# Nine diagonal matrices for the first norm, made by VectorE in place of ScalarE

## The chip, the cores and the metric

The kernel runs on one core of one Trainium2 chip. The metric is the device time of one execution in microseconds (us), as the median of several runs. The times are taken without the profiler; one more execution is recorded by the hardware profiler, and it is the one that the views show.

## What is computed

The reference is one step of a one-layer hybrid encoder, for 1024 prompt frames and 32 sample frames (1056 columns in all), model width 1024. Cut to what matters here:

```python
def rmsnorm(x, g):
    y = xf * lax.rsqrt(jnp.mean(xf * xf, axis=-1, keepdims=True) + EPS)
    return y * g

h = rmsnorm(x, g_mix)
proj = h @ w_in
q, k, v, cb, cc, cx, ga, gc = jnp.split(proj, SPLITS, axis=-1)
...
```

What follows (attention, a short convolution, gates, an output projection, a squared-ReLU MLP, a gated embedding and a last norm) is not touched by the change.

## The kernel before

The data are kept by feature: features lie on the 128 partitions, frames along the columns. The first norm is not applied ahead of the projection. The kernel multiplies the weights with `x * g_mix`, and scales each finished product by the frame's factor 1/rms, which must then stand in every partition: the tile `rs`, 128 x 1056. Its making is the place of the change.

The functions `stats_x` (L397) and `spread` (L384) make it. `stats_x` takes nine blocks of frames by rows (eight of 128, one of 32), lets ScalarE sum the squares of each (L403, into a column of `ssq`), takes the root on ScalarE (L408) and the reciprocal on VectorE (L409). The result `rst` has a frame per partition and a block per column. `spread` is then called three times, for three blocks each. For a block it scales the identity by the block's column of `rst`, which gives a diagonal matrix `dg` (L391), and multiplies it with a matrix of ones on TensorE (L392), which puts each frame's factor into all partitions of a column of the PSUM tile `pr`. When the three blocks of a call are there, ScalarE copies `pr` into `rs` (L394). The tile `dg` has four buffers and `pr` two. An fp32 matmul shows as two passes in the trace, so nine blocks give 18 records.

The order of the work is written by hand: within `manual_schedule` every engine runs its instructions in the order of the program. The main work is a list of matrix products, `seven` (L208), seven block products per pair of weight tiles, with each product's sum split in a high and a low part (three matmuls, L202 to L204). The output of a product leaves PSUM through a copy of ScalarE (L227, L231, L235, L647) or an operation of VectorE (L238, L243, L248). After each product, `run` advances every generator in the list `side` by one step: `prepare` makes the next weights' parts (adds on GpSimd, L189; casts on ScalarE, L150 and L97; differences on VectorE, L152 and L98), `fetch_in` issues loads on SyncE's queue (L88), and `stats_x` is one of these generators too. All three calls of `spread` lie in its last step, between two products of `seven`: behind the copy L231 of the second product `S1` and ahead of the product into `ps_A11i` that follows.

At the end of the kernel, `diagonals` (L1635) and `everywhere` (L1644) do the same for the later norms in blocks of 100 or 128 frames (L1641, L1649); the change doesn't touch them. The function `inv_rms`, which calls `spread` too, isn't used.

Of the kernel before, what the change touches and what calls it, by code (L numbers as in the profile page):

```python
# [11 lines left out]
AF = mybir.ActivationFunctionType  # L12
ALU = mybir.AluOpType
# [35 lines left out]
def tile_step(  # L49
# [8 lines left out]
    nc = tc.nc  # L58
# [13 lines left out]
    ident = cpool.tile([P, P], F32, name="ident")  # L72
# [311 lines left out]
    def spread(r9, dst, q0):  # L384

        w = min(3 * P, T - q0 * P)
        pr = tps.tile([P, 512], F32, tag="tp", name="pr")
        for i in range(q0, q0 + 3):
            n = P if i < 8 else DEC
            dg = cpool.tile([P, P], F32, tag="dg", name="dg", bufs=4)  # L390
            nc.scalar.activation(dg, ident, AF.Copy, scale=r9[:, i : i + 1])  # L391
            nc.tensor.matmul(pr[:, (i - q0) * P : (i - q0) * P + n], ones, dg[:, :n], start=True, stop=True)  # L392
        if dst is not None:
            nc.scalar.copy(dst[:, q0 * P : q0 * P + w], pr[:, :w])  # L394
        return pr[:, :w]

    def stats_x():  # L397

        nc.vector.memset(ssq, 1.0)
        for i in range(9):  # L400
            n = P if i < 8 else DEC
            r = rows[i % 3][:n, :]
            nc.scalar.activation(r, r, AF.Square, accum_out=ssq[:n, i : i + 1])  # L403
            if i < 6:
                load_rows(i + 3)
            for _ in range(3 if i in (2, 5) else 1):
                yield
        nc.scalar.activation(rst, ssq, AF.Sqrt, bias=eps_t, scale=1.0 / D)  # L408
        nc.vector.reciprocal(rst, rst)  # L409
        for _ in range(3):  # L410
            yield
        for q0 in (0, 3, 6):
            spread(rst, rs, q0)
# [668 lines left out]
    with tc.manual_schedule(engines=MM):  # L1082
# [3 lines left out]
        for n in range(len(steps) + 3):  # L1086
            done_f, parts = 0, None
            w0, w1 = (pace_ + [FILL])[n : n + 2]
            if n < len(steps):
                i = steps[n][2]  # L1090
# [53 lines left out]
    def inv_rms(src, r, name, square=False):  # L1144
        r9 = cpool.tile([P, 9], F32, name=f"r9{name}")
        nc.vector.memset(r9, 1.0)
        row_rms(src, r9, range(9), name, square)
        for q0 in (0, 3, 6):
            spread(r9, r, q0)
# [793 lines left out]
```

## Time and profile before

| | us |
|---|---|
| median of 3 runs | 1547.47 |
| lowest and highest | 1547.33, 1547.64 |
| the profiled execution | 1547.13 |
| its span in the profile | 1545.4 |
| mean granted clock of TensorE | 0.998 |

The span runs from the first to the last instruction; the profiled execution's own time is 1.7 us longer, which lies around the span. In the views, PE is TensorE, PEld its weight loads, DVE is VectorE, ACT is ScalarE, POOL is GpSimd and SP is SyncE, which issues the transfers. Tiles are shown by name without their number, so the product tiles of this stage are `ps_A11i`, `ps_A12i` and `ps_S1i`. A bracket at the end of a line of the timeline tells how long the engine was idle before it and whose instruction ended that. Ends of matmuls are modelled and overlap the next start, so the pace of TensorE is read from starts.

### The profile page before, as it was taken

Reading aid. Unit: us, or ns where it says so; the run is one execution under the profiler, and the core shown is the slowest. Engines: PE = TensorE matmul, PEld = TensorE weight load, DVE = VectorE, ACT = ScalarE, POOL = GpSimd, SP = SyncE. Lnnn points to the kernel's source line nnn. Section 1 sums busy time; section 2 is a strip of 40 time slices with the busy share of each in tenths; the row PEclk is TensorE's granted clock in tenths of the full one; section 3 lists DMA queues with packets and bytes.
Section 4 is the critical chain, followed back from the end, with each engine's and each line's share of the span. In section 5 each row is a group of like instructions: output and inputs, shape, how many; then the busy total and the mean of one; then the engine's idle time right before and its main releaser. Section 6 shows DMA issues by size and latency. Waiting matters only on the chain.

```text
span 1545.4 us, 29349 instructions
## 1 busy us (share of the span) xinstructions
PE 1521.4 (98%) x11786; PEld 1507.2 (98%) x11786; DVE 1058.1 (68%) x1385; ACT 759.7 (49%) x1393; POOL 347.2 (22%) x294
## 2 busy tenths in 40 slices
PE   8999999999999999999999999999999999999997
PEld 8999999999999999999999999999999999999997
DVE  7524686667688887766577555544576986789856
ACT  6652344443566775333355555555543333434656
POOL 1122232230211114002312222221020221013453
PEclk9999999999999999999999999999999999999999
DMA  6522245534735576235454344344886897683443
GB/s 243 180 93 84 56 166 193 205 132 121 224 113 156 157 229 236 90 137 170 162 189 145 143 150 151 132 142 154 282 303 202 275 337 242 195 282 108 141 133 111
DMA packets 111559, 269.10 MB, mean 174 GB/s; under 512 B 13472, under 2 KB 29216, under 8 KB 111424
## 3 DMA queue, kind: packets, MB, share of 16 engines
q1 hardware_dynamic: 110704, 265.05, 51.0%
q8 instruction: 92, 1.51, 0.4%
q10 hardware_dynamic: 720, 2.19, 0.4%
q14 instruction: 43, 0.35, 0.1%
HBM read 186.46 MB, written 80.73 MB: 173 GB/s over the span
## 4 chain that ended last, share of the span: by engine, by line
PE 92%; DVE 4%; ACT 2%; issue 1%; DMA 0%; SPq 0%; POOL 0%; DVEq 0%; ACTq 0%; POOLq 0%
PE ps_dn L1473 7%; PE ps_dn L1472 7%; PE ps_dn L1474 7%; PE ps_A11u L203 4%; PE ps_A11u L202 4%; PE ps_A11u L204 4%; PE ps_A11i L202 4%; PE ps_A11i L204 4%; PE ps_A11i L203 4%; PE av L874 2%; PE ps_wo L106 2%; PE ps_wo L107 2%; PE ps_wo L108 2%; PE ps_S1u L203 2%; PE ps_S1u L202 2%; PE ps_S1u L204 2%
## 5 line engine op out<-in xcount | busy, mean ns | idle before, releaser
L1473 PE MATMUL ps_dn<-fl,whi_dn 128*128 128x264 f32 x896 | 254.8, 284 | 0.1
L1474 PE MATMUL ps_dn<-fh,wlo_dn 128*128 128x264 f32 x896 | 254.9, 284 | 0.0
L1472 PE MATMUL ps_dn<-fh,whi_dn 128*128 128x264 f32 x896 | 254.8, 284 | 0.0
L1473 PEld LDWEIGHTS ps_dn<-fl,whi_dn 128*128 128x128 f32 x896 | 168.5, 188 | 0.3 <-DVE fl L1381 0.3
L1472 PEld LDWEIGHTS ps_dn<-fh,whi_dn 128*128 128x128 f32 x896 | 168.6, 188 | 0.0
L1474 PEld LDWEIGHTS ps_dn<-fh,wlo_dn 128*128 128x128 f32 x896 | 168.6, 188 | 0.0
L189 POOL TENSOR_TENSOR s_i<-raw_i,raw_i 128x512 f32<-128x512 f32 x30 | 40.4, 1346 | 232.8 <-DVE slS_i L152 210.4
L1365 DVE TENSOR_TENSOR wlo_dn<-raw_dn,whi_dn 128x1024 fp32r<-128x1024 f32 x40 | 71.0, 1774 | 25.7 <-ACT whi_dn L1359 25.1
L1359 ACT CAST whi_dn<-raw_dn 128x1024 fp32r<-128x1024 f32 x40 | 42.1, 1052 | 93.7 <-PE ps_dn L1473 79.5
L819 DVE TENSOR_TENSOR_SCAN r<-r 128x128 f32<-128x128 f32 (+3 forms) x64 | 86.6, 1354 | 2.1 <-POOL r L812 2.1
L189 POOL TENSOR_TENSOR s_u<-raw_u,raw_u 128x512 f32<-128x512 f32 x30 | 44.7, 1491 | 186.3 <-DVE slS_u L152 185.6
L1414 POOL TENSOR_TENSOR c<-c,rs 128x528 f32<-128x528 f32 x16 | 26.7, 1669 | 244.1 <-DVE c L1481 122.6
L1381 DVE TENSOR_TENSOR fl<-mr,fh 128x1056 fp32r<-128x1056 f32 x56 | 69.7, 1247 | 4.1 <-ACT fh L1376 4.1
L152 DVE TENSOR_TENSOR slS_i<-s_i,shS_i 128x512 fp32r<-128x512 f32 x45 | 36.0, 802 | 49.2 <-ACT shS_i L150 49.0
L202 PE MATMUL ps_A11i<-T,shS_i 128*128 128x264 f32 x240 | 69.0, 287 | 0.2 <-ACT u_i L235 0.2
L203 PE MATMUL ps_A11i<-T,shS_i 128*128 128x264 f32 x240 | 68.6, 286 | 0.0
L204 PE MATMUL ps_A11i<-T,slS_i 128*128 128x264 f32 x240 | 68.4, 285 | 0.0
L202 PE MATMUL ps_A11u<-T,shS_u 128*128 128x264 f32 x240 | 68.4, 285 | 0.0
L203 PE MATMUL ps_A11u<-T,shS_u 128*128 128x264 f32 x240 | 68.3, 285 | 0.0
L204 PE MATMUL ps_A11u<-T,slS_u 128*128 128x264 f32 x240 | 68.1, 284 | 0.0
L812 POOL TENSOR_SCALAR_AFFINE_SELECT r<-r 128x128 f32<-128x128 f32 x64 | 26.6, 416 | 165.2 <-ACT r L805 165.1
L1376 ACT CAST fh<-mr 128x1056 fp32r<-128x1056 f32 x56 | 60.1, 1073 | 5.0 <-DMA mr<-mdB 5.0
(462 smaller groups left out, 5591.8 us busy)
## 6 DMA issues: line engine op xcount, KB each, us to landing
raw_dn<-in_w_down_dram SPq DMA_DIRECT2D x56, 512.0 KB, 4.7
raw_i<-in_w_in_dram SPq DMA_DIRECT2D x34, 512.0 KB, 4.4
mr<-mdT SPq DMA_DIRECT2D x32, 528.0 KB, 5.4
raw_u<-in_w_up_dram SPq DMA_DIRECT2D x32, 512.0 KB, 3.5
mdB<-m SPq DMA_DIRECT2D x48, 264.0 KB, 2.4
mr<-mdB SPq DMA_DIRECT2D x24, 528.0 KB, 6.5
s<-gd SPq DMA_DIRECT2D x16, 528.0 KB, 5.4
mdT<-ta SPq DMA_DIRECT2D x32, 264.0 KB, 2.1
```

Source lines behind the costliest of these rows:

```text
L189: f()
L202: nc.tensor.matmul(p_, wh[:, k, :], o[:, 0, c], start=new and n == 0, stop=False, **on)
L203: nc.tensor.matmul(p_, wh[:, k, :], o[:, 1, c], start=False, stop=False, **on)
L204: nc.tensor.matmul(p_, wl[:, k, :], o[:, 0, c], start=False, stop=z, **on)
L819: nc.vector.tensor_tensor_scan(rev, rev, rev, 1.0, ALU.mult, ALU.bypass)
L1359: nc.scalar.copy(hi, dws[u])
L1365: dve(lo, raw, hi.bitcast(F32), op=sub)
L1376: nc.scalar.copy(h, mraw[v])
L1381: dve(l, mraw.pop(v), opd[v].bitcast(F32), op=sub)
L1472: nc.tensor.matmul(ps, hi[:, j, :], oh, start=j == 0, stop=False)
L1473: nc.tensor.matmul(ps, hi[:, j, :], ol, start=False, stop=False)
L1474: nc.tensor.matmul(ps, lo[:, j, :], oh, start=False, stop=j == NP_ - 1)
```

## The change

One line of `spread` is replaced. The scaled identity is made by VectorE's `tensor_scalar` with a multiply, from the same operands, instead of ScalarE's `activation` with a scale. Nothing else is changed: the position in the program, the four buffers of `dg`, the matmuls and the copies stay. VectorE's nine instructions take the place of ScalarE's nine in the program's order.

```diff
             dg = cpool.tile([P, P], F32, tag="dg", name="dg", bufs=4)
-            nc.scalar.activation(dg, ident, AF.Copy, scale=r9[:, i : i + 1])
+            nc.vector.tensor_scalar(dg, ident, r9[:, i : i + 1], None, op0=ALU.mult)
             nc.tensor.matmul(pr[:, (i - q0) * P : (i - q0) * P + n], ones, dg[:, :n], start=True, stop=True)
```

## The prediction

> **What bounds the kernel now.** I read the page first, then the waits of TensorE, then the order of time around the edited line. The page:
>
> ```profile
> span 1545.4 us, 29349 instructions
> ...
> PE 1521.4 (98%) x11786; PEld 1507.2 (98%) x11786; DVE 1058.1 (68%) x1385; ACT 759.7 (49%) x1393; POOL 347.2 (22%) x294
> ...
> PE 92%; DVE 4%; ACT 2%; issue 1%; DMA 0%; SPq 0%; POOL 0%; DVEq 0%; ACTq 0%; POOLq 0%
> ```
>
> TensorE is busy for 98% of the span, and 92% of the chain that ended last is its work. So time that TensorE loses anywhere is lost at the end, and the question is only what it loses at the nine diagonals. The waits of TensorE between 84 and 300 us have one large entry (total, times, longest), and it is the edited line:
>
> ```profile
> PE pr L392 <- ACT dg L391: 2.5, 3, 0.9
> ```
>
> Those 2.5 us are idle time only. Inside the three groups TensorE also runs at the pace of the diagonals, which the timeline shows (start, duration, engine, line):
>
> ```profile
> 83.79 0.29 PE L203 MATMUL ps_S1i<-T,shS_i 128*128 128x264 f32 x1
> 83.91 0.28 PE L204 MATMUL ps_S1i<-T,slS_i 128*128 128x264 f32 x1
> 84.23 0.38 ACT L231 COPY s_i<-ps_S1i 128x264 f32<-128x264 f32 x1 [1.08 <-PE ps_S1i L204]
> 84.50 0.98 ACT L391 ACTIVATE dg<-ident,rst 128x128 f32<-128x128 f32 x3
> 84.96 1.07 PE L392 MATMUL pr<-dg,ones 128*128 128x128 f32 x6 [0.77 <-ACT dg L391]
> 86.07 0.48 ACT L394 COPY rs<-pr 128x384 f32<-128x384 f32 x1 [0.58 <-PE pr L392]
> 86.44 0.98 ACT L391 ACTIVATE dg<-ident,rst 128x128 f32<-128x128 f32 x3
> 86.90 1.07 PE L392 MATMUL pr<-dg,ones 128*128 128x128 f32 x6 [0.87 <-ACT dg L391]
> 88.00 0.48 ACT L394 COPY rs<-pr 128x384 f32<-128x384 f32 x1 [0.58 <-PE pr L392]
> 88.38 0.98 ACT L391 ACTIVATE dg<-ident,rst 128x128 f32<-128x128 f32 x3
> 88.84 1.49 PE L392 MATMUL pr<-dg,ones 128*128 128x128 f32 x6 [0.87 <-ACT dg L391]
> 90.14 0.57 PE L202 MATMUL ps_A11i<-T,shS_i 128*128 128x264 f32 x1
> ```
>
> This is a ping-pong. ScalarE can begin the diagonals only after its copy of the product just finished (L231), makes three, waits until TensorE has used them, copies the result out (L394), and only then makes the next three. The products before follow each other every 0.12 us (83.79 to 83.91), so TensorE could have gone on at 84.03; the next product starts at 90.14. The stretch costs 6.11 us for 18 passes (each fp32 matmul is two).
>
> A second loss follows. The windows show the granted clock (length, PE busy, PEclk, DMA share, GB/s), and two starts of products bound it:
>
> ```profile
> 88.60:88.80 0.20, 0.00 (x0) 1.00 0.00 0
> 88.80:89.00 0.20, 0.16 (x1) 0.53 0.00 0
> 92.00:92.20 0.20, 0.20 (x3) 0.50 0.00 0
> 92.20:92.40 0.20, 0.20 (x4) 0.94 0.00 0
> ...
> 92.25 0.29 PE L202 MATMUL ps_A11i<-T,shS_i 128*128 128x264 f32 x1
> 94.08 0.28 PE L202 MATMUL ps_A12i<-B,whi_i 128*128 128x264 f32 x1
> ```
>
> From 88.8 to 92.2 us the clock is at half. From 92.25 to 94.08 stand 15 starts, 0.122 us each; the nine before them, from 90.14 to 92.25, took 2.11 us in place of 9 x 0.122 = 1.10. So the drop cost 1.01 us after the stretch, besides what it cost within it.
>
> **The change part by part.** It removes nine instructions of ScalarE and puts nine of VectorE in the same place of the program:
>
> ```profile
> L391 ACT ACTIVATE dg<-ident,rst x9: 388/389/403, 84.5 to 89.0; 128x128 f32<-128x128 f32 x9
> L1680 DVE TENSOR_SCALAR yl<-yl,r 128x512 f32<-128x512 f32 x1 | 0.5, 486 | 0.0
> L1682 DVE TENSOR_SCALAR yl<-yl,r 128x256 f32<-128x256 f32 x2 | 0.7, 346 | 0.0
> L555 DVE TENSOR_SCALAR cs<-ce,vecT 128x2 f32<-128x2 f32 x4 | 0.9, 221 | 0.0
> ```
>
> *One diagonal on VectorE.* No row has this operation at 128 columns. From 256 to 512 columns it grows by 140 ns, so 128 columns give 346 - 70 = 276 ns. The bounds are the rows of 2 columns (221 ns) and of 512 (486 ns). I take 0.28 us, for both neighbours lie on that line.
>
> *When they can start.* VectorE's timeline around the place, with POOL's:
>
> ```profile
> 80.66 0.21 DVE L409 RECIPROCAL rst<-rst 128x9 f32<-128x9 f32 x1 [1.09 <-ACT rst L408]
> 81.17 0.69 DVE L152 TENSOR_TENSOR slS_i<-s_i,shS_i 128x512 fp32r<-128x512 f32 x1 [0.29 <-ACT shS_i L150]
> 93.75 0.69 DVE L152 TENSOR_TENSOR slA_i<-raw_i,shA_i 128x512 fp32r<-128x512 f32 x1 [11.89 <-ACT shA_i L150]
> ...
> 82.00 1.28 POOL L189 TENSOR_TENSOR s_i<-s_i,raw_i 128x512 f32<-128x512 f32 x1 [1.00 <-DVE slS_i L152]
> 102.72 1.28 POOL L189 TENSOR_TENSOR s_i<-raw_i,raw_i 128x512 f32<-128x512 f32 x1 [19.43 <-DVE slS_i L152]
> ```
>
> The factor is ready at 80.87, and VectorE idles from 81.86 to 93.75. Its next work, the L152 of 93.75, needs a cast that ScalarE issues after the spread, so the diagonals are queued ahead of it. Four buffers hold diagonals, so four are made from about 81.9 to 83.0, while TensorE still multiplies. The first three waits go; they are covered by VectorE's idle time.
>
> *What is late next.* A fully fed pass is seen at the end of the kernel, where the diagonals are all made before the matmuls start:
>
> ```profile
> 1445.09 0.34 PE L108 MATMUL ps_pg<-bh,wlo_pg 128*128 128x400 f32 x1
> 1445.27 1.03 PE L1649 MATMUL pr<-dg,ones 100*128 100x100 f32 x8
> ...
> L1649 PE MATMUL pr<-dg,ones x36: 249/275/353, 1445.3 to 1519.1; 100*128 100x100 f32 x32, 128*128 128x128 f32 x4
> ```
>
> Eight passes in 1.03 us with 0.275 for one: (1.03 - 0.275)/7 = 0.108 us between starts. With 128 columns it may be up to the 0.12 of the products. From 84.03, 18 x 0.108 = 1.94 us end at 85.97; by 0.12, at 86.19. Two waits can remain in it:
> - The fifth diagonal needs the buffer of the first, that is the end of pass 2 (84.14 + 0.275 = 84.41). With 0.05 us to VectorE, 0.28 for itself and 0.07 to TensorE (84.96 less the first diagonal's end at 84.50 + 0.39), it is there at 84.81; pass 9 is due at 84.89. The others follow every 0.28 while a pair of passes takes 0.216: the ninth, there at 85.93, is about 0.06 late.
> - The third group writes the buffer of the first, which ScalarE must have copied out (two buffers): pass 6 ends at 84.57 + 0.275 = 84.85, the copy takes 0.48 from 84.89 to 85.37, TensorE may write at 85.44, and pass 13 is due at 85.33. Cost 0.11.
>
> These overlap, so the next product starts at about 86.1 instead of 90.14: **4.0 us** gained. Bounds: 4.16 with no wait and 0.108; and, with the 0.49 of the 512-column row for a diagonal, the ninth is there at 84.46 + 5 x 0.49 + 0.07 = 86.98, the product starts at 87.2, and 2.9 are gained.
>
> *The clock.* The drop came at 88.8, and in the 3.4 us before it TensorE sat idle twice for 0.87. Fed without those gaps, passes keep the clock:
>
> ```profile
> 1445.00:1448.00 3.00, 3.00 (x27) 2.96 (x26) 2.61 (x6) 2.16 (x6) 0.00 (x0) 1.00 0.41 99
> ```
>
> Here the same kind of passes ran with clock 1.00. I take it that the drop goes: another **1.0 us**. Bounds: from a full drop that stays (3.4 us at half, 1.7 lost: 0.7 worse than now) to 1.0 gained. Here a rule of the Trainium skill speaks against me: "TensorE: Matmul & The Clock Gate", Part 1, says that the clock is halved after an idle window of about 3.4 us, and that the windows run free of the kernel. The length agrees (88.8 to 92.2 is 3.4 us), the cause does not quite: the longest idle here was 0.87 us. By that rule the waits did not cause the drop and it would stay, which is my second case.
>
> *What lies behind.* ScalarE loses nine times about 0.3 us here, of no worth in itself; its copies follow TensorE. Does the gain survive to the end? At the stretch the kernel has run dry:
>
> ```profile
> 84.00:94.00 10.00, 7.49 (x44) 6.92 (x43) 0.25 (x1) 5.56 (x16) 0.00 (x0) 0.83 0.00 0
> ...
> 94.47 1.85 SPq L88 DMA_DIRECT2D raw_i<-in_w_in_dram  x2
> ```
>
> DMA share 0.00, POOL nothing, VectorE nothing before 93.75, and the next loads wait for buffers that VectorE frees. All that follows hangs on TensorE's products, so it moves as one block. POOL's add of 82.00 lies beside the first diagonals; if one waits for the other, a diagonal is up to 1.28 us late: then the fourth is there at 83.28 + 4 x 0.28 + 0.07 = 84.47, due at 84.68, and nothing is lost.
>
> **Sum.** 4.0 + 1.0 = 5.0 us. The profiled execution took 1547.13 (1.7 beyond its span), so 1542.1; by the median of the runs, 1547.47, it is 1542.5. I take the middle, **1542.3 us**, 0.33% less.
>
> **The rivals.**
> 1. *The clock still drops.* The pauses go, but a 3.4 us stretch at half clock falls on dense products and loses 1.7: gain 5.0 - 1.7 = 3.3, so 1543.8 to 1544.2. For: the passes use narrow tiles, and what the clock looks at isn't seen. Against: the row of 1445 with clock 1.00.
> 2. *The diagonals pace TensorE.* At 0.49 us each, gain 2.9 + 1.0 = 3.9, so 1543.2 to 1543.6. For: the fifth waits for a buffer. Against: two rows put it at 0.28.
> 3. *The lead is given back.* A later wait that doesn't move eats over 1.9 us, leaving the time above 1544.4. For: TensorE does wait elsewhere in 1540 us. Against: everything was idle at the stretch, so no transfer or engine was ahead that could now be caught up with.
> 4. *Slower.* Each of diagonals five to nine waits out one add of POOL (1.28, as the row of 82.00) before its own 0.28. Then the ninth is there at 84.46 + 5 x 1.56 + 0.07 = 92.3, the product starts at 92.5, 2.4 us later than now: 1549.5. It decides from 1.1 us each (84.46 + 5 x 1.1 = 90). Against: POOL has one add between 82.00 and 102.72. The Trainium skill, "SBUF — State Buffer", Who interferes with whom, states that such an operation of VectorE and any of GpSimd can shut each other out of a shared port for a whole instruction; no row here shows these two side by side.
>
> **How the numbers follow.** A measurement of this kernel can tell about 0.2%, 3.1 us, from no change: below 1544.4 counts as faster. Chances: the forecast 0.68, the dropping clock 0.13, the pacing 0.11, the lead given back 0.06, slower 0.02. The first three are all faster (0.92). The range runs from 1540.9 (4.16 + 1.0, and up to 1 us more where a run's drop fell wholly on dense products) to 1544.2, the upper ends of rivals 1 and 2.
>
> **What the next profile would show.** Nine DVE instructions at L391 of about 0.28 us, four before 83.1; one unbroken group of 18 passes from 84.0 with no wait over 0.2; the next product near 86.1; the granted clock 1.00 from 86 to 93; the two copies L394 near 84.9 and 86; span near 1540.4. Wrong would be: a diagonal of 0.4 or more with waits of TensorE on VectorE, a half-clock window behind 86, or an equal span with a new wait between the stretch and the end.

## The result

The changed kernel takes 1542.91 us (median of 8 runs, 1542.00 to 1543.91); the kernel before, measured beside it, 1547.95 (8 runs, 1546.15 to 1549.15). The ratio is 0.9967, with a 95% interval from 0.9957 to 0.9978: 5.0 us faster, clear of no change. The profiled execution took 1543.23 us, with a span of 1541.5. The forecast was 1542.3 us and a gain of 5.0.

### The profile page after: what moved, and what is told of

Its sections match the earlier page's. It is cut to its first block, busy times and chain, and to the rows that moved or that the text cites. A ratio compares the mean times of both kernels' runs of the same rounds, so it can differ in the third digit from the quotient of the medians.

```text
span 1541.5 us, 29349 instructions
## 1 busy us (share of the span) xinstructions
PE 1520.1 (99%) x11786; PEld 1506.4 (98%) x11786; DVE 1061.1 (69%) x1394; ACT 756.8 (49%) x1384; POOL 347.1 (23%) x294
## 4 chain that ended last, share of the span: by engine, by line
PE 92%; DVE 4%; ACT 2%; issue 1%; DMA 0%; SPq 0%; POOL 0%; DVEq 0%; ACTq 0%; POOLq 0%
PE ps_dn L1473 7%; PE ps_dn L1472 7%; PE ps_dn L1474 7%; PE ps_A11u L203 4%; PE ps_A11u L202 4%; PE ps_A11u L204 4%; PE ps_A11i L202 4%; PE ps_A11i L204 4%; PE ps_A11i L203 4%; PE av L874 2%; PE ps_wo L106 2%; PE ps_wo L107 2%; PE ps_wo L108 2%; PE ps_S1u L203 2%; PE ps_S1u L202 2%; PE ps_S1u L204 2%
## 5 line engine op out<-in xcount | busy, mean ns | idle before, releaser
L1473 PE MATMUL ps_dn<-fl,whi_dn 128*128 128x264 f32 x896 | 255.0, 285 | 0.1
L1473 PEld LDWEIGHTS ps_dn<-fl,whi_dn 128*128 128x128 f32 x896 | 168.6, 188 | 0.3 <-DVE fl L1381 0.3
```

The source lines that it names most:

```text
L1473: nc.tensor.matmul(ps, hi[:, j, :], ol, start=False, stop=False)
```

## The profile after

The page of the changed kernel has nine instructions more on VectorE and nine fewer on ScalarE, and TensorE's share is up by a point:

```profile
span 1541.5 us, 29349 instructions
...
PE 1520.1 (99%) x11786; PEld 1506.4 (98%) x11786; DVE 1061.1 (69%) x1394; ACT 756.8 (49%) x1384; POOL 347.1 (23%) x294
```

The timeline around the edited line, of all engines (start, duration, engine, line):

```profile
82.45 1.90 DVE L391 TENSOR_SCALAR dg<-ident,rst 128x128 f32<-128x128 f32 x4
82.67 1.40 POOL L189 TENSOR_TENSOR s_i<-s_i,raw_i 128x512 f32<-128x512 f32 x1 [1.00 <-DVE slS_i L152]
...
84.59 0.28 PE L204 MATMUL ps_S1i<-T,slS_i 128*128 128x264 f32 x1
84.71 2.25 PE L392 MATMUL pr<-dg,ones 128*128 128x128 f32 x18
85.12 1.18 DVE L391 TENSOR_SCALAR dg<-ident,rst 128x128 f32<-128x128 f32 x5 [0.78 <-PE pr L392]
85.57 0.48 ACT L394 COPY rs<-pr 128x384 f32<-128x384 f32 x1 [0.29 <-PE pr L392]
86.24 0.48 ACT L394 COPY rs<-pr 128x384 f32<-128x384 f32 x1 [0.19 <-PE pr L392]
...
86.80 0.37 PE L202 MATMUL ps_A11i<-T,shS_i 128*128 128x264 f32 x1
87.00 0.40 ACT L394 COPY rs<-pr 128x288 f32<-128x288 f32 x1 [0.27 <-PE pr L392]
...
89.80 0.29 PE L202 MATMUL ps_A12i<-B,whi_i 128*128 128x264 f32 x1
```

Where three groups of six passes stood with a pause ahead of each, one group of 18 stands, with one short wait inside it: fed passes start every 0.11 us (84.71 to 85.93 for the first twelve), and the 13th, the first of the third group, starts at 86.11, 0.06 us late, behind the first copy (85.57 + 0.48 = 86.05). Four diagonals are ready before TensorE reaches them. From the last start of the product `S1` to the next product it is 86.80 - 84.59 = 2.21 us, where it was 90.14 - 83.91 = 6.23: **4.02 us** gone (0.47 of it by the third group, whose last passes ran at half clock before: 1.30 us from its start to the next product in before, 0.83 where the clock holds, as in e4 below). The 24 starts behind it, from 86.80 to 89.80, take 3.00 us, where they took 3.94 (90.14 to 94.08): **0.94 us** gone. The windows tell why (length; busy time and count of PE, PEld, DVE, ACT, POOL; granted clock, DMA share, GB/s):

```profile
86.00:93.00 7.00, 7.00 (x59) 6.91 (x59) 2.64 (x6) 3.58 (x8) 0.00 (x0) 1.00 0.23 73
```

The clock is 1.00 throughout. Together 4.96 us are gained in this place. The span is only 3.9 us shorter, since in this execution the product `S1` ended 0.68 us later than in that of before, ahead of the changed place, and 0.4 us differ in the 1450 us behind it. The lead holds to the end. The row of the later norms' matmuls, of the changed kernel, has the first start at 1441.3, where it was 1445.3 before, and the last at 1515.2, where it was 1519.1:

```profile
L1649 PE MATMUL pr<-dg,ones x36: 249/275/353, 1441.3 to 1515.2; 100*128 100x100 f32 x32, 128*128 128x128 f32 x4
```

## The experiments

Two theories stand against each other. **Theory 1**: the loss was one of place. The diagonals stood in ScalarE's queue behind copies that wait for TensorE, so the two engines took turns, and the pauses brought the clock down. **Theory 2**: the engine counts, because VectorE's instruction is shorter (0.28 against 0.39 us) or because ScalarE has less to do. For each kernel I give the time from the last start of `S1` to the next product ("stretch") and to the first start of `ps_A12i`, 24 starts later ("with products"); before has 6.23 and 10.17, the changed kernel 2.21 and 5.21.

### e1: the diagonals stay on ScalarE, earlier in its queue

Nothing is left out; the diagonals are written into row tiles that are no longer used, so none waits for a buffer.

```diff
+    ready = []
+    def make_ready(*blocks):
+        for i in blocks:
+            dg = rows[i // 8][:, i % 8 * P : (i % 8 + 1) * P]
+            nc.scalar.activation(dg, ident, AF.Copy, scale=rst[:, i : i + 1])
+            ready.append(dg)
...
-        for _ in range(3):
-            yield
+        for q0 in (0, 3, 6):
+            yield
+            make_ready(q0, q0 + 1, q0 + 2)
```

In `spread`, `dg = ready[i]` takes the place of the two lines that made it.

> The nine diagonals stay on ScalarE, with the same instruction, but stand earlier in its queue: three behind each of the three products ahead of the spread, written into the row tiles that are free by then, so none waits for a buffer. Theory 1 (place in the queue: the diagonals stood behind copies that wait for TensorE, and the pauses brought the clock down): the first two groups run without a wait; the first copy L394 stands behind the last three diagonals (to about 85.9 on the scale of before), so the third group is some 0.6 late; the next product starts 2.6 to 2.8 us after the last start of S1 in place of 6.2; the clock keeps 1.00; 4.2 to 4.7 us faster than before, about 1543.5. Theory 2 (the engine: VectorE's diagonal is shorter and ScalarE has less to do): ScalarE does the same work in the same time, so under 1 us is gained, 1547 to 1548.

Measured: 1543.96 us (1543.41 to 1544.48), ratio to before 0.9967, 0.9954 to 0.9979; before in these runs 1549.24. Stretch 2.69 (84.42 to 87.11), with products 5.69. The timeline of e1:

```profile
82.09 0.99 ACT L401 ACTIVATE xr<-ident,rst 128x128 f32<-128x128 f32 x3
...
83.55 0.99 ACT L401 ACTIVATE xr<-ident,rst 128x128 f32<-128x128 f32 x3
84.54 1.50 PE L391 MATMUL pr<-xr,ones 128*128 128x128 f32 x12
...
85.02 0.98 ACT L401 ACTIVATE xr<-ident,rst 128x128 f32<-128x128 f32 x3
85.90 0.84 ACT L393 COPY rs<-pr 128x384 f32<-128x384 f32 x2
86.42 0.85 PE L391 MATMUL pr<-xr,ones 128*128 128x128 f32 x6 [0.38 <-ACT rs L393]
```

ScalarE does as many diagonals, each as long as before, and nearly all of the gain is there. By the medians it is 5.3 us, more than the 4.2 to 4.7 expected, since most runs of before beside it have a mean clock of 0.996. Theory 2 falls. The one wait left, 0.38 us, is that of the third group for the first copy, which stands behind the last three diagonals: place in the queue again.

### e7: nine on ScalarE at the old place, ahead of the copies

As e1, with `make_ready(*range(9))` at the place of the old diagonals.

> All nine diagonals on ScalarE at the place of before, but ahead of the three copies instead of three and three between them, into row tiles that are free. Theory 1 (place in the queue): the first pause stays (0.77), TensorE is then paced by a diagonal every 0.3 us, the first copy stands behind the ninth diagonal (87.2 on the scale of before) and the third group behind that copy (87.7): 4.4 to 4.6 us from the last start of S1 to the next product in place of 6.2, so 1.7 us faster where before's clock does not drop (1546.4), 1544.5 to 1545.5. Theory 2 (the engine): ScalarE's work is unchanged, so the time of before.

Measured: 1544.95 us (1544.38 to 1546.77), ratio 0.9982, 0.9973 to 0.9991; before in these runs 1548.65. Stretch 4.43 (83.93 to 88.36), with products 7.44.

```profile
84.52 2.74 ACT L401 ACTIVATE xr<-ident,rst 128x128 f32<-128x128 f32 x9
84.98 1.95 PE L391 MATMUL pr<-xr,ones 128*128 128x128 f32 x12 [0.77 <-ACT xr L401]
87.16 0.83 ACT L393 COPY rs<-pr 128x384 f32<-128x384 f32 x2
87.67 0.85 PE L391 MATMUL pr<-xr,ones 128*128 128x128 f32 x6 [0.75 <-ACT rs L393]
```

Same engine, same nine instructions; what differs is their order among the copies, and that they are written into free row tiles, so nine can be made without a buffer to wait for. The stretch is 1.80 us shorter than in the profile of before, and 1.32 shorter than in e2 (5.75), which takes the old turns at full clock. The first pause stays, since the first diagonal is still behind the copy of `S1`; a second stands where the copy is late. The clock stayed at 1.00 with two pauses of 0.77 and 0.75 us (more on that below).

### e4: only the first call's diagonals on VectorE

```diff
+            if q0 == 0:
+                nc.vector.tensor_scalar(dg, ident, r9[:, i : i + 1], None, op0=ALU.mult)
+            else:
+                nc.scalar.activation(dg, ident, AF.Copy, scale=r9[:, i : i + 1])
```

> Only the first call's three diagonals are made by VectorE; the other six stay on ScalarE. Theory 1: the first group starts with no wait and with no gap inside, the first copy L394 and the two calls behind it come 1.2 us earlier, and their two pauses stay: the stretch is 5.0 in place of 6.2 us. Whether two pauses bring the clock down is open: 1.2 us faster than before if it drops, 2.2 to 2.6 if it doesn't; 1545.3 to 1546.8. Theory 2 (the work taken off ScalarE counts): a third of 5.0, 1.7 us, spread evenly, with the first pause as long as before.

Measured: 1544.98 us (1544.73 to 1545.77), ratio 0.9977, 0.9966 to 0.9987; before 1549.24. That is 4.3 us by the medians, more than expected; the time itself lies just under the expected range. In the profile the stretch is 4.58 (85.08 to 89.66) and with products 7.58, so 2.59 us less than in the profile of before: the second group starts 1.81 after the last start of `S1` where it was 2.99 (1.18, as forecast), and the clock gives 0.47 in the third group and 0.94 behind it. The rest of the 4.3 lies in the runs of before, whose clock drop mostly costs more than in its profile (below). The waits of TensorE for ScalarE are now two:

```profile
PE pr L395 <- ACT dg L394: 1.7, 2, 0.9
```

### e3: one buffer for the diagonals

```diff
+    one = [cpool.tile([P, P], F32, tag="dg", name="dg", bufs=4)]
...
-            dg = cpool.tile([P, P], F32, tag="dg", name="dg", bufs=4)
+            dg = one[0]
```

> The changed kernel with a single buffer for the diagonals, so each waits until TensorE has used the one before. The prediction's terms for a round trip: 0.07 to TensorE, 0.108 to the second pass, 0.275 for it, 0.05 back, 0.28 for the diagonal, about 0.78 us for each. Theory 1: nine on VectorE in this order cost 8 x 0.78 + 0.22 = 6.5 us from the last start of S1 to the next product, 0.3 more than before, and with TensorE busy for 0.22 of 0.78 the clock drops again and may stay low for two windows of 3.4 us: 1547.5 to 1550. Theory 2 (the engine): the instructions and their engine are those of the changed kernel, so its 1543 stays within 1 us.

Measured: 1550.62 us (1550.15 to 1552.08), ratio to before 1.0013, 1.0004 to 1.0022, so 7.7 above the changed kernel. VectorE does the same nine instructions and the whole gain is lost, and more. Stretch 7.55 (84.95 to 92.50), with products 12.97. One round of it in the timeline:

```profile
85.83 0.49 PE L394 MATMUL pr<-dg,ones 128*128 128x128 f32 x2 [0.38 <-DVE dg L393]
86.36 0.28 DVE L393 TENSOR_SCALAR dg<-ident,rst 128x128 f32<-128x128 f32 x1 [0.58 <-PE pr L394]
86.69 0.49 PE L394 MATMUL pr<-dg,ones 128*128 128x128 f32 x2 [0.38 <-DVE dg L393]
```

The windows of e3 in which the clock falls and rises again:

```profile
91.00:92.00 1.00, 0.58 (x2) 0.30 (x2) 0.32 (x2) 0.00 (x0) 0.00 (x0) 0.68 0.00 0
...
97.00:98.00 1.00, 1.00 (x7) 1.00 (x6) 0.75 (x2) 0.36 (x1) 0.00 (x0) 0.50 0.00 0
98.00:99.00 1.00, 1.00 (x9) 1.00 (x9) 0.62 (x1) 0.84 (x2) 0.00 (x0) 0.91 0.63 139
```

A round takes 0.86 us, not the 0.78 of the prediction's terms: the hand-overs are 0.04 and 0.05 us and the diagonal 0.28, but a pair of passes that starts on an idle TensorE takes 0.49 instead of 0.108 + 0.275. The stretch is so 1.0 us longer than the 6.5 expected, and the time lies 0.6 above the expected range. The clock is at half from about 91.4 to 98.2, 6.8 us, twice the length seen before. The prediction's slower rival is another mechanism (it needed POOL's adds); what e3 shows is that a round trip that TensorE must wait out can cost more than the old turn-taking.

### e2: the pauses filled, not shortened

Four matmuls are added ahead of each group; their result is overwritten.

```diff
+        for _ in range(4):
+            nc.tensor.matmul(pr[:, :P], ones, ident, start=True, stop=True)
```

> The kernel before, with four additional matmuls of the ones and the identity into pr ahead of each group of three, overwritten by the real ones, to fill TensorE's pauses without shortening them (four fp32 matmuls are eight passes, 0.86 us by 0.108; the pauses are 0.77 to 0.87). Theory 1 (the pauses bring the clock down): the three waits for ScalarE stay but the clock stays at 1.00; the 24 products behind the stretch take 2.95 us in place of 3.94 and the third group 1.07 in place of 1.49, together 1.4 us faster than before, about 1546.5. Rival (the clock drops for another reason than the pauses): half clock for 3.4 us appears as before, the same time as before or up to 1 us longer.

Measured: 1546.61 us (1546.29 to 1548.14), ratio 0.9986, 0.9978 to 0.9995; before 1549.24. Stretch 5.75 (84.14 to 89.89), with products 8.75: 1.42 us less than in the profile of before, by the clock alone. The timeline of e2:

```profile
84.26 1.05 PE L389 MATMUL pr<-ident,ones 128*128 128x128 f32 x8
...
84.74 0.98 ACT L393 ACTIVATE dg<-ident,rst 128x128 f32<-128x128 f32 x3
85.19 1.07 PE L394 MATMUL pr<-dg,ones 128*128 128x128 f32 x6
86.10 1.06 PE L389 MATMUL pr<-ident,ones 128*128 128x128 f32 x8
```

And the window of it in which the clock of before fell:

```profile
88.00:90.00 2.00, 2.00 (x17) 1.83 (x17) 0.00 (x0) 1.36 (x4) 0.00 (x0) 1.00 0.00 0
```

The turn-taking goes on as before, every diagonal at its old time, and the clock holds. Ten of the eleven runs of e2 have a mean clock of 0.999; of the 24 runs of before beside them, three have it. So the pauses did bring the clock down, and its cost is separate from theirs.

### e5, e9, e10, e11: the kernel before again

The times of before spread over 4 us. In one set of 21 runs beside the second group of experiments they follow the mean granted clock: 1546.1 us at 0.999 (three runs), 1547.1 to 1548.7 at 0.998 (six), 1548.5 to 1549.4 at 0.996 and 0.997 (twelve). Elsewhere the order is looser: three runs of e5 at 0.997 took 1547.2 to 1547.4 us, and e2 spreads from 1546.3 to 1548.1 with 0.999 in ten of eleven runs, so some of the spread has another place, which no trace here shows. These four runs of the unchanged kernel look for the place of the clock's part.

> The kernel before, unchanged, in another execution. Its runs lie between 1546.4 us at a mean granted clock of 0.999 and 1550.3 at 0.996. Theory 1 on the clock (the pauses bring it down, but what it costs depends on where the 3.4 us windows fall): same groups and the same 6.2 us from the last start of S1 to the next product within 0.4, but a half-clock stretch that begins elsewhere or lasts two windows (6.8 us) where the mean clock is 0.996 or 0.997, with up to 3.4 us lost on the products behind. Rival (the spread of the times comes from another place): the same stretch of 3.4 us as before, and the difference in span lies elsewhere.

> The kernel before, unchanged, one more look, in search of an execution whose mean granted clock is 0.996 or 0.997. Theory 1 on the clock: if it is 0.996, half clock lasts about 6.8 us here (two stretches of 3.4), the products behind the stretch lose about 3 us and the span is near 1547.5; if 0.998, one stretch as in the profile of before. Rival: at 0.996 the half-clock time lies elsewhere in the kernel.

> The kernel before, unchanged, one more look with the same question: two stretches of 3.4 us at half clock behind the pauses where the mean clock is 0.996, one where it is 0.998, none where it is 0.999.

> The kernel before, unchanged, one more look with the same question: two stretches of 3.4 us at half clock behind the pauses where the mean clock is 0.996, one where it is 0.998, none where it is 0.999.

Measured: e5 1547.29 us (median of 10 runs, ratio to the other runs of before 0.9994, 0.9985 to 1.0003), the others one execution each.

| | time of the profiled run | mean clock | stretch | with products | half clock |
|---|---|---|---|---|---|
| profile of before | 1547.13 | 0.998 | 6.23 | 10.17 | 88.8 to 92.2 |
| e5 | 1547.03 | 0.998 | 6.02 | 10.24 | about 88.9 to 92.3 |
| e11 | 1548.07 | 0.998 | 5.91 | 10.30 | about 89.8 to 93.2 |
| e9 | 1549.25 | 0.997 | 6.67 | 11.22 | about 87.8 to 94.6 |
| e10 | 1549.22 | 0.996 | 6.54 | 11.25 | about 88.2 to 95.0 |

The two ends of the half clock in the windows of e10:

```profile
88.00:89.00 1.00, 1.00 (x6) 0.74 (x4) 0.00 (x0) 0.19 (x1) 0.00 (x0) 0.60 0.00 0
89.00:90.00 1.00, 0.13 (x2) 0.10 (x1) 0.00 (x0) 0.93 (x3) 0.00 (x0) 0.50 0.00 0
94.00:95.00 1.00, 1.00 (x6) 1.00 (x6) 0.00 (x0) 0.77 (x2) 0.00 (x0) 0.50 0.00 0
95.00:96.00 1.00, 1.00 (x10) 1.00 (x9) 0.69 (x1) 1.00 (x2) 0.00 (x0) 0.98 0.00 0
```

The clock is at half for 3.4 us or for 6.8. Against e2, which has the same turns at full clock (8.75), the drop costs 1.4 to 1.6 us in the one case and 2.5 in the other, its share within the groups included. Behind the stretch, the 24 starts take 4.55 us in e9 and 4.71 in e10 in place of 3.00, so they lose 1.6 and 1.7 us, not the 3 expected. In e9 and e10 the clock falls within the second group, so that the pause ahead of the third lies in the first 3.4 us at half clock, as a pause of e3 does; in the other three traces at most 0.03 us of a pause is left when it falls. An execution of before with 0.999 has no trace here; that its clock never drops in this place is inferred from its time, 1546.1, which is near that of e2's fastest (1546.29).

### e6: the diagonals of VectorE made at once

All nine are made on VectorE behind the reciprocal, into the row tiles, as in e1 with `nc.vector.tensor_scalar` and `make_ready(*range(9))` ahead of the three `yield`.

> The changed kernel with all nine diagonals made at once behind the reciprocal, ahead of L152, into row tiles that are free; none waits for a buffer, and they are done before POOL's add starts. Theory 1: what is left of the stretch is the matmuls themselves, so from the last start of S1 to the next product 2.05 to 2.2 us in place of 2.21; same time as the changed kernel within 0.5 us. On the long diagonal (1.31 us beside POOL's add): if POOL causes it, no diagonal is above 0.35 here, apart from one beside the end of POOL's add before; if it is something of the third or first instruction of its kind, it comes again.

Measured: 1542.19 us (1541.78 to 1543.53), ratio 0.9963, 0.9950 to 0.9975; the changed kernel in the same set (e8) 0.9965, 0.9952 to 0.9977. Stretch 2.21 (85.10 to 87.31), with products 5.21, the same as the changed kernel to the hundredth. So the making of the diagonals costs nothing any more. What is left of the stretch is the matmuls and the short wait of the third group, which is here too (the first copy ends at 86.08 + 0.48 = 86.56, the 13th pass starts at 86.62), and e6 is not faster by anything that can be told here. Its diagonals, and those of e8:

```profile
L401 DVE TENSOR_SCALAR xr<-ident,rst x9: 276/278/288, 82.3 to 83.9; 128x128 f32<-128x128 f32 x9
```

```profile
L391 DVE TENSOR_SCALAR dg<-ident,rst x9: 276/286/1311, 82.8 to 86.3; 128x128 f32<-128x128 f32 x9
```

In e6 POOL's add starts at 84.93, after the last diagonal, and none is long (the add before it ends at 82.41, as the first diagonal, of 82.33, begins). In the changed kernel the add stands beside them (at 82.67 in its first profile): the third diagonal takes 1.31 us, and the add 1.40 in place of 1.28. The third is the long one in both profiles of the changed kernel and in e4; that it is short in e6 points to the add, not to its place in the row.

### e8: the changed kernel again

> The changed kernel again, beside the others on one chip: within 1 us of 1543, clock 0.999 in every run, 2.2 us from the last start of S1 to the next product.

Measured: 1542.75 us (1542.40 to 1543.12), ratio to the 1548.65 of before 0.9965, 0.9952 to 0.9977. Stretch 2.21 (84.89 to 87.10), with products 5.22. The mean clock was 0.999 in three runs and 0.998 in two, the profiled one among them; its trace shows 1.00 in every microsecond from 83 to 99, so the difference lies elsewhere: at the end of the kernel, where TensorE has no more work, the clock falls to half at 1535.9 and stays there for 5.5 us to the end of the span; in the first profile of the changed kernel it falls at 1538.5, 3.0 us before the end.

## Why the prediction was right

- **That TensorE's time is the kernel's time**: right. The lead of the stretch is there at 1098 us (the first matmul of L1473 starts at 1098.6 in place of 1102.6) and at 1441 us, and TensorE's waits show no new entry that took it. The third rival (the lead given back) doesn't appear.
- **The pauses, 4.0 us**: right, 4.02. On the scale of after (0.68 later) the fifth diagonal was forecast to start at 85.14 and started at 85.12, the first copy at 85.57 and it did, the next product at 86.8 and it did. Of the two waits in the sum, the third group's for the first copy is there, 0.06 us late where 0.11 was forecast, and the pass behind it starts another 0.10 late (0.21 behind the 13th). The ninth diagonal's, forecast 0.06 late, is not: the diagonals overlap and start every 0.22 us, not every 0.28, so the ninth was ready at 86.02 + 0.29 = 86.31 and its pass came at 86.65. A pass takes 0.111 us in place of 0.108, and the last block, only 32 columns wide, saves 0.08. That the product's start was met to 0.02 us is thus the luck of small errors that cancel; the mechanism and the size of 4 us are not. The mechanism is shown by e1 and e7: the same instructions on ScalarE at other places in its queue give most of the gain or some of it.
- **A diagonal on VectorE, 0.28 us**: right (276 to 288 ns where POOL is idle), so the second rival, diagonals that pace TensorE, falls.
- **POOL's add beside the first diagonals**: the mechanism was right and its cost nil, as forecast. The four first diagonals were done at 82.45 + 1.90 = 84.35, and the fourth was due, six passes of 0.111 behind 84.71, at 85.37. The page of the Trainium skill that was named for it, "SBUF — State Buffer", Who interferes with whom, has the one that starts later wait for the whole instruction of the other. The trace agrees: the long diagonal starts at 82.84, inside the add (82.67 to 84.07), and ends at 84.15; in e6, where no add stands beside them, none is long. The slower rival needed one add for each of five diagonals, and there was one in all.
- **The clock, 1.0 us**: right in kind, and right in size for the profile (0.94), but the size was drawn from one execution. With the share within the groups it runs from nothing, by inference, over 1.4 (the profile) to 2.5 us in the executions of before. So that the medians differ by just the 5.0 forecast is partly luck, the mix of those runs (both medians lie 0.5 to 0.6 us above the numbers that the forecast used and gave): in the set where before had 1548.65, the changed kernel had 1542.75 (e8), 5.9 less.
- **The rule that spoke against it**: "TensorE: Matmul & The Clock Gate", Part 1, in the Trainium skill names an idle window of about 3.4 us as what halves the clock. The length of the drop agrees (3.4 us and twice that). The condition does not: here TensorE was busy for half of the 3.4 us ahead of the drop (1.7 to 1.8 us in all six traces with one), and e2 shows that filling these pauses of under 0.9 us keeps the clock. Three rows: the 3.4 us ahead of the drop in the profile of before; the 3.4 us of e4 that hold most of its pauses; and 3.4 us near the end of e9, behind which the clock stayed at 1.00:

```profile
85.40:88.80 3.40, 1.70 (x11) 1.31 (x10) 0.00 (x0) 2.24 (x8) 0.00 (x0) 1.00 0.00 0
...
85.06:88.47 3.41, 2.03 (x15) 1.65 (x13) 0.00 (x0) 2.21 (x7) 0.00 (x0) 1.00 0.00 0
...
1538.46:1541.87 3.41, 1.54 (x14) 1.34 (x12) 2.54 (x10) 2.84 (x4) 0.00 (x0) 1.00 0.29 113
```

What the clock goes by stays open, but the traces narrow it. In the six traces with a drop, half clock lasts 3.41 or 6.83 us, and full clock from there to the fall at the kernel's end 1450.66 or 1447.25 us. These are 1, 2, 425 and 424 times 3.413 us, so I infer that the clock is set anew every 3.413 us, on one grid through a run. Counted back from their falls at the end (1539.14 and 1540.50), the grid of e4 has most of its pauses in one step with 2.03 us of busy time, and that of e7 spreads its pauses over two steps with 2.64 and 2.67; both kept the clock. By this, where the grid falls decides what the same pauses cost. Busy time alone is not the condition, though: the step of e9 above has only 1.54 us, of 14 matmuls of 256 columns, and kept the clock; the step behind it (1541.87 to 1545.29), with no work of TensorE at all, brought it down.

## What to carry to other kernels

When two engines hand small tiles back and forth, look at what stands ahead of the producer's instructions in its own queue: a copy that waits for the consumer turns three short hand-overs into turn-taking. An idle engine is one way out; the same engine with the work issued earlier, into space that is already free, gave most of the same gain. And count the clock: pauses of under a microsecond in a row can halve TensorE's clock for 3.4 or 6.8 us after them, so a kernel whose runs spread by a few us may be showing the luck of that drop; the mean granted clock of each run is a first hint, and a trace of a run with a low one shows the place.

## What the runs showed of the hardware beyond what was expected

- Half clock came in stretches of 3.4 us or 6.8 us, after 3.4 us in which TensorE was half busy, with no pause over 0.9 us (in e3 none over 0.5).
- Two passes of an fp32 128x128 matmul that start on an idle TensorE took 0.49 us at full clock (e3); fed one behind the other, passes started every 0.111 us (the first twelve of the changed kernel, 84.71 to 85.93).
- A `tensor_scalar` of 128x128 fp32 on VectorE took 0.28 us alone, with a start every 0.20 us (e6, nine from 82.33 to 83.91), and 1.31 us beside an add on GpSimd, which itself took 1.40 in place of 1.28.
